# Record count of a projected sequence, one core: broadcast of w over TensorE, last tiles in halves, scans in the tail

## Chip, cores, metric

One core of a Trainium2 chip. The metric is device time in microseconds of one execution, median of several; lower is better. All runs told here were in the fast state. A profile adds a span (first to last instruction), some 1.8 us shorter than the measured time (2.1 us in one kernel, halves_only).

## Reference

```python
def reference(x, w):                      # x: 8 x 2048 x 4096 fp32, w: 4096 x 1 fp32
    proj = (x @ w).squeeze(-1)            # 8 x 2048
    cm = np.maximum.accumulate(proj, axis=1)
    is_record = (proj >= cm).astype(np.float32)
    return np.cumsum(is_record, axis=1).astype(np.float32)
```

x is 268 MB and is read once, each value used once. What follows the projection is a running maximum and a running count over 2048 values in each of 8 sequences.

## The kernel before

x is read in 128 tiles of 128 rows (2.10 MB each) into six buffers. VectorE multiplies each with w, which a broadcast DMA has laid on all 128 partitions, and sums into one column.

```python
w_sb = const.tile([P, D], FP32)
nc.gpsimd.dma_start(out=w_sb, in_=w[:, 0].partition_broadcast(P))   # 2.10 MB
for t in range(T):
    xtile = xpool.tile([P, D], FP32, tag="x")                       # bufs=6
    nc.sync.dma_start(out=xtile, in_=xt[t])
    nc.vector.scalar_tensor_tensor(out=xtile, in0=xtile, scalar=1.0, in1=w_sb,
        op0=ALU.mult, op1=ALU.mult, accum_out=proj_all[:, t : t + 1])
```

Then the tail. proj_all is transposed, so that row t holds the 128 values of tile t. Scans along the rows are made of doubling steps, the carry from row to row goes through a transpose, four more steps in one lane and a transpose back.

```python
projT = copy(transpose(proj_all))
def l1_scan(bufA, bufB, src, op):                 # 7 steps, k = 1, 2, 4 ... 64
    ...
        nc.vector.tensor_tensor(out=nxt[:, PAD:], in0=cur[:, PAD:],
                                in1=cur[:, PAD - k : PAD + P - k], op=op)
def cross_carry(rowval_col, scA, scB, op):
    nc.vector.tensor_copy(out=ZCOL[:, 0:1], in_=rowval_col)
    nc.tensor.transpose(out=p1, in_=ZCOL, identity=ident)
    ...                                           # copy, 4 steps in one lane, copy
    nc.tensor.transpose(out=p2, in_=ZROW, identity=ident)
    return p2[:, 0:1]
cmbuf = l1_scan(MA, MB, projT, ALU.max)
carry_m = cross_carry(last column of cmbuf, ..., ALU.max)
...                                               # compare, 7 steps of add, cross_carry, final add
nc.sync.dma_start(out=out_r, in_=res)
```

## Time and profile before

| quantity | before | from |
|---|---|---|
| time | 659.09 us (4 runs, 658.77 to 659.57); 659.2 to 659.3 beside later runs | timed runs |
| span | 657.2 us | profile |
| first multiply starts | 15.89 us | timeline |
| multiply of the last tile starts | 637.41 us | timeline |
| output DMA issued | 654.63 us | timeline |
| stream rate | 428 GB/s | windows |

The views of this profile are shown and read in the prediction below. In short: DMA sets the pace up to the last tile, VectorE is 88% busy but keeps up, and after the last tile one chain of VectorE and TensorE steps runs with no transfer beside it.

### The profile page before, as it was taken

The page shows a single profiled execution, that of the slowest core. Times are in us where ns is not written, and L with a number is a line of the kernel's source. Part 1 is how long each engine was busy: PE and PEld are TensorE (multiplying, and loading weights), DVE is VectorE, ACT ScalarE, POOL GpSimd, SP SyncE. Part 2 cuts the span into 40 slices and gives each one's busy share as a digit, 9 for nine tenths or more (in the row PEclk, how much of TensorE's full clock was granted, in tenths as well). Part 3 has the DMA queues.
Part 4 walks back from the last instruction along what each step waited for, and adds up shares of the span by engine and source line. Part 5 has one row for each costly group of instructions (what it writes and reads, how often), then busy time and mean ns, then how long its engine had stood idle before and what let it go on. Part 6 is the DMA issues. An engine that isn't in the chain of part 4 may idle for free.

```text
span 657.2 us, 739 instructions
## 1 busy us (share of the span) xinstructions
PE 2.3 (0%) x5; PEld 0.9 (0%) x5; DVE 577.3 (88%) x297; ACT 1.5 (0%) x2; POOL 1.4 (0%) x7
## 2 busy tenths in 40 slices
PE   0000000000000000000000000000000000000001
PEld 0000000000000000000000000000000000000000
DVE  1999898899899899899899899899998899898995
ACT  0000000000000000000000000000000000000000
POOL 0000000000000000000000000000000000000000
DMA  9999999999999999999999999999999999999950
GB/s 366 430 431 428 428 427 427 430 429 430 427 428 427 430 429 429 428 428 428 428 429 428 428 430 429 427 429 430 428 428 429 426 429 430 427 428 429 430 251 4
DMA packets 18725, 270.65 MB, mean 412 GB/s; under 512 B 2080, under 2 KB 2208, under 8 KB 2208
## 3 DMA queue, kind: packets, MB, share of 16 engines
q1 hardware_dynamic: 18576, 268.51, 96.1%
q0 software_dynamic: 144, 2.10, 0.7%
q14 instruction: 5, 0.04, 0.0%
HBM read 270.53 MB, written 0.07 MB: 412 GB/s over the span
## 4 chain that ended last, share of the span: by engine, by line
DMA 82%; DVE 17%; issue 1%; PE 0%; DVEq 0%; ACT 0%; POOLq 0%
DMA xtile<-in_x_dram 79%; DVE xtile L58 16%; DMA w_sb<-in_w_dram 2%; DVE NB L154 0%; DVE MB L103 0%; PE p L116 0%; PE p L135 0%; DVE NA L154 0%; DVE MA L103 0%; DVE SC_S_B L124 0%; DVE SC_M_A L124 0%; DVE SC_M_B L124 0%; DVE SC_S_A L124 0%; PE pt_ps L69 0%; DVE ZROW L133 0%
## 5 line engine op out<-in xcount | busy, mean ns | idle before, releaser
L58 DVE SCALAR_TENSOR_TENSOR xtile<-xtile,w_sb 128x4096 f32<-128x4096 f32 x128 | 566.1, 4425 | 72.2 <-DMA xtile<-in_x_dram 58.8
L58 DVE DVE_READ_ACCUMULATOR xtile<-xtile,w_sb 128x1 f32 x128 | 10.6, 83 | 0.0
L69 PE MATMUL pt_ps<-ident,proj_all 128*128 128x128 f32 x1 | 0.4, 446 | 642.0 <-DVE xtile L58 642.0
L71 ACT COPY projT<-pt_ps 128x128 f32<-128x128 f32 x1 | 0.3, 266 | 640.4 <-PE pt_ps L69 640.4
L103 DVE TENSOR_TENSOR MB<-MA 128x128 f32<-128x128 f32 x4 | 1.2, 292 | 0.1
L154 DVE TENSOR_TENSOR NB<-NA 128x128 f32<-128x128 f32 x4 | 1.2, 292 | 0.1
L71 ACT ACT_TABLE_LOAD x1 | 1.3, 1283 | 0.7 <-PEq L190 0.7
L69 PEld LDWEIGHTS pt_ps<-ident,proj_all 128*128 128x128 f32 x1 | 0.2, 181 | 642.0 <-issue 642.0
L99 DVE COPY MA<-projT 128x128 f32<-128x128 f32 x1 | 0.2, 227 | 0.9 <-ACT projT L71 0.9
L103 DVE TENSOR_TENSOR MA<-MB 128x128 f32<-128x128 f32 x3 | 0.9, 292 | 0.1
L154 DVE TENSOR_TENSOR NA<-NB 128x128 f32<-128x128 f32 x3 | 0.9, 292 | 0.1
L116 PE MATMUL p<-ident,ZCOL 128*128 128x128 f32 x2 | 0.9, 461 | 6.1 <-DVE ZCOL L114 6.1
L142 DVE SCALAR_TENSOR_TENSOR NA<-MB,p,projT 128x128 f32<-128x128 f32 x1 | 0.4, 357 | 0.6 <-PE p L135 0.6
L135 PE MATMUL p<-ident,ZROW 128*128 128x128 f32 x2 | 0.9, 446 | 3.9 <-DVE ZROW L133 3.9
L167 DVE TENSOR_SCALAR res<-NB,p 128x128 f32<-128x128 f32 x1 | 0.3, 292 | 0.6 <-PE p L135 0.6
L79 DVE MEMSET MA<- 128x64 f32 x1 | 0.1, 112 | 0.8 <-PEq L190 0.8
L118 DVE COPY SC_S_A<-p 1x120 f32<-1x120 f32 x1 | 0.3, 270 | 0.6 <-PE p L116 0.6
L118 DVE COPY SC_M_A<-p 1x120 f32<-1x120 f32 x1 | 0.3, 269 | 0.6 <-PE p L116 0.6
L48 POOL DMA_DIRECT2D w_sb<-in_w_dram x1 | 0.7, 660 | 0.8 <-POOLq L190 0.8
L124 DVE TENSOR_TENSOR SC_S_B<-SC_S_A 1x128 f32<-1x128 f32 x2 | 0.6, 280 | 0.1
L124 DVE TENSOR_TENSOR SC_M_B<-SC_M_A 1x128 f32<-1x128 f32 x2 | 0.6, 279 | 0.1
L124 DVE TENSOR_TENSOR SC_M_A<-SC_M_B 1x128 f32<-1x128 f32 x2 | 0.6, 279 | 0.1
(22 smaller groups left out, 4.7 us busy)
## 6 DMA issues: line engine op xcount, KB each, us to landing
xtile<-in_x_dram SPq DMA_DIRECT2D x128, 2048.0 KB, 24.8
w_sb<-in_w_dram POOLq DMA_DIRECT2D x1, 2048.0 KB, 14.6
out_dram<-res SPq DMA_DIRECT2D x1, 64.0 KB, 1.5
```

What stands on the lines that cost most here:

```text
L48: nc.gpsimd.dma_start(out=w_sb, in_=w_flat.partition_broadcast(P))
L58: nc.vector.scalar_tensor_tensor(out=xtile, in0=xtile, scalar=1.0, in1=w_sb, op0=ALU.mult, op1=ALU.mult, accum_out=proj_all[:, t : t + 1],)
L69: nc.tensor.transpose(out=pt_ps, in_=proj_all, identity=ident)
L71: nc.scalar.copy(out=projT, in_=pt_ps)
L103: nc.vector.tensor_tensor(out=nxt[:, PAD:], in0=cur[:, PAD:], in1=cur[:, PAD - k : PAD + P - k], op=op,)
L116: nc.tensor.transpose(out=p1, in_=ZCOL, identity=ident)
L118: nc.vector.tensor_copy(out=scA[:, :, SO + 1 : 2 * SO], in_=rowv[:, :, 0 : SO - 1])
L124: nc.vector.tensor_tensor(out=nxt[:, :, SO:], in0=cur[:, :, SO:], in1=cur[:, :, SO - k : 2 * SO - k], op=op,)
L135: nc.tensor.transpose(out=p2, in_=ZROW, identity=ident)
L142: nc.vector.scalar_tensor_tensor(out=NA[:, PAD:], in0=cmbuf[:, PAD:], scalar=carry_m, in1=projT, op0=ALU.max, op1=ALU.is_le,)
L154: nc.vector.tensor_tensor(out=nxt[:, PAD:], in0=cur[:, PAD:], in1=cur[:, PAD - k : PAD + P - k], op=ALU.add,)
L167: nc.vector.tensor_scalar(out=res, in0=csbuf[:, PAD:], scalar1=carry_s, scalar2=None, op0=ALU.add,)
```

## The change

It aims at both ends of the stream. (1) w is loaded as one row of 16 KB, spread over the partitions by eight fp32 matmuls with a row of ones, and copied to SBUF by ScalarE. (2) The last six tiles are loaded and multiplied in halves, so that less is left to do after the last bytes. (3) The tail uses VectorE's scan instruction, and of the four transposes that carried values from row to row one stays, while two matmuls with one column replace the other three (one of the two with a triangle matrix that sums the row counts). Cut to its core:

```diff
-    nc.gpsimd.dma_start(out=w_sb, in_=w_flat.partition_broadcast(P))
+    nc.scalar.dma_start(out=w_row, in_=w[:, 0][None, :])
+    for j in range(D // MM_N):                     # 8 times 512 columns
+        nc.tensor.matmul(wp, lhsT=ones_row, rhs=w_row[:, j * MM_N : (j + 1) * MM_N], start=True, stop=True)
+        nc.scalar.copy(out=w_sb[:, j * MM_N : (j + 1) * MM_N], in_=wp)
+    LASTT = 6
+    Q = 2
     for t in range(T):
+        if t < T - LASTT: ...                      # whole tile, as before
+        for q in range(Q):
+            cs = slice(q * W, (q + 1) * W)
+            nc.sync.dma_start(out=xtile[:, cs], in_=xt[t][:, cs])
+            nc.vector.scalar_tensor_tensor(out=xtile[:, cs], in0=xtile[:, cs], scalar=1.0,
+                in1=w_sb[:, cs], op0=ALU.mult, op1=ALU.mult,
+                accum_out=parts[:, t - (T - LASTT), q : q + 1])
+    nc.vector.tensor_reduce(out=proj_all[:, T - LASTT :], in_=parts, op=ALU.add, axis=AX.X)
     nc.tensor.transpose(out=pt_ps, in_=proj_all, identity=ident)
-    (copy to SBUF, copy, 7 steps, copy, transpose, copy, 4 steps, copy, transpose)
+    nc.vector.tensor_tensor_scan(out=CM, data0=NEGT, data1=pt_ps, initial=NEG_INF, op0=ALU.max, op1=ALU.max)
+    nc.tensor.transpose(out=p1[0:1, :], in_=CM[:, P - 1 : P], identity=ident)
+    nc.vector.tensor_copy(out=SC[:, :, 1:SO], in_=rowv[:, :, 0 : SO - 1])
+    nc.vector.tensor_tensor_scan(out=ZR, data0=RST..., data1=SC..., initial=NEG_INF, op0=ALU.min, op1=ALU.max)
+    nc.tensor.matmul(p2[:, 0:1], lhsT=ZR, rhs=ones_row[0:1, 0:1], start=True, stop=True)
     (compare)
-    (7 steps, copy, transpose, copy, 4 steps, copy, transpose)
+    nc.vector.tensor_tensor_scan(out=CS, data0=ONES, data1=REC, initial=0.0, op0=ALU.mult, op1=ALU.add)
+    nc.tensor.matmul(p3[:, 0:1], lhsT=Mtri2, rhs=CS[:, P - 1 : P], start=True, stop=True)
     (final add, output)
```

More of the change, by code (lines that the diff above doesn't have):

```diff
@@ L44 @@
     psum = ctx.enter_context(tc.tile_pool(name="psum", bufs=2, space=bass.MemoryType.PSUM))
-    w_sb = const.tile([P, D], FP32)
-    w_flat = w[:, 0]
-    nc.gpsimd.dma_start(out=w_sb, in_=w_flat.partition_broadcast(P))
+    psumw = ctx.enter_context(tc.tile_pool(name="psumw", bufs=4, space=bass.MemoryType.PSUM))
     ident = const.tile([P, P], FP32)
     make_identity(nc, ident)
+    w_row = const.tile([1, D], FP32)
+    nc.scalar.dma_start(out=w_row, in_=w[:, 0][None, :])
+    ones_row = const.tile([1, P], FP32)
@@ new lines @@
+    nc.vector.memset(ones_row, 1.0)
+    w_sb = const.tile([P, D], FP32)
+    MM_N = 512
+    for j in range(D // MM_N):
+        wp = psumw.tile([P, MM_N], FP32, tag="wp")
+        nc.tensor.matmul(
+            wp, lhsT=ones_row, rhs=w_row[:, j * MM_N : (j + 1) * MM_N],
+            start=True, stop=True,
+        )
+        nc.scalar.copy(out=w_sb[:, j * MM_N : (j + 1) * MM_N], in_=wp)
+    Mtri = const.tile([P, B, SO], FP32)
+    nc.gpsimd.memset(Mtri, 1.0)
+    nc.gpsimd.affine_select(
+        out=Mtri, in_=Mtri, compare_op=ALU.is_ge, fill=0.0,
+        base=-1, pattern=[[SO, B], [1, SO]], channel_multiplier=-1,
+    )
@@ L53 @@
+    nc.gpsimd.affine_select(
+        out=Mtri, in_=Mtri, compare_op=ALU.is_ge, fill=0.0,
+        base=0, pattern=[[-SO, B], [0, SO]], channel_multiplier=1,
+    )
+    Mtri2 = Mtri.rearrange("k b j -> k (b j)")
     proj_all = small.tile([P, T], FP32)
+    LASTT = 6
+    Q = 2
+    W = D // Q
+    parts = small.tile([P, LASTT, Q], FP32)
     for t in range(T):
         xtile = xpool.tile([P, D], FP32, tag="x")
-        nc.sync.dma_start(out=xtile, in_=xt[t])
-        nc.vector.scalar_tensor_tensor(
-            out=xtile,
-            in0=xtile,
-            scalar=1.0,
-            in1=w_sb,
-            op0=ALU.mult,
-            op1=ALU.mult,
-            accum_out=proj_all[:, t : t + 1],
-        )
+        if t < T - LASTT:
+            nc.sync.dma_start(out=xtile, in_=xt[t])
+            nc.vector.scalar_tensor_tensor(
+                out=xtile, in0=xtile, scalar=1.0, in1=w_sb,
+                op0=ALU.mult, op1=ALU.mult, accum_out=proj_all[:, t : t + 1],
+            )
+            continue
+        for q in range(Q):
+            cs = slice(q * W, (q + 1) * W)
+            nc.sync.dma_start(out=xtile[:, cs], in_=xt[t][:, cs])
+            nc.vector.scalar_tensor_tensor(
+                out=xtile[:, cs], in0=xtile[:, cs], scalar=1.0, in1=w_sb[:, cs],
+                op0=ALU.mult, op1=ALU.mult,
+                accum_out=parts[:, t - (T - LASTT), q : q + 1],
+            )
@@ L68 @@
+    nc.vector.tensor_reduce(
+        out=proj_all[:, T - LASTT :], in_=parts, op=ALU.add, axis=AX.X,
+    )
     pt_ps = psum.tile([P, P], FP32, tag="tp")
     nc.tensor.transpose(out=pt_ps, in_=proj_all, identity=ident)
-    projT = small.tile([P, P], FP32, tag="projT")
-    nc.scalar.copy(out=projT, in_=pt_ps)
-    PAD = P // 2
-    MA = small.tile([P, PAD + P], FP32, tag="MA")
-    MB = small.tile([P, PAD + P], FP32, tag="MB")
-    NA = small.tile([P, PAD + P], FP32, tag="NA")
-    NB = small.tile([P, PAD + P], FP32, tag="NB")
@@ L79 @@
-    nc.vector.memset(MA[:, :PAD], NEG_INF)
-    nc.vector.memset(MB[:, :PAD], NEG_INF)
-    nc.vector.memset(NA[:, :PAD], 0.0)
-    nc.vector.memset(NB[:, :PAD], 0.0)
-    SC_M_A = small.tile([1, B, 2 * SO], FP32, tag="scma")
-    SC_M_B = small.tile([1, B, 2 * SO], FP32, tag="scmb")
-    SC_S_A = small.tile([1, B, 2 * SO], FP32, tag="scsa")
-    SC_S_B = small.tile([1, B, 2 * SO], FP32, tag="scsb")
-    nc.vector.memset(SC_M_A, NEG_INF)
-    nc.vector.memset(SC_M_B, NEG_INF)
-    nc.vector.memset(SC_S_A, 0.0)
@@ L91 @@
-    nc.vector.memset(SC_S_B, 0.0)
-    ZCOL = const.tile([P, P], FP32)
-    ZROW = const.tile([P, P], FP32)
-    nc.vector.memset(ZCOL, 0.0)
-    nc.vector.memset(ZROW, 0.0)
-    def l1_scan(bufA, bufB, src, op):
-        nc.vector.tensor_copy(out=bufA[:, PAD:], in_=src)
-        cur, nxt = bufA, bufB
-        k = 1
-        while k < P:
-            nc.vector.tensor_tensor(
-                out=nxt[:, PAD:],
-                in0=cur[:, PAD:],
-                in1=cur[:, PAD - k : PAD + P - k],
-                op=op,
-            )
-            cur, nxt = nxt, cur
-            k *= 2
-        return cur
@@ L113, in cross_carry @@
-    def cross_carry(rowval_col, scA, scB, op):
-        nc.vector.tensor_copy(out=ZCOL[:, 0:1], in_=rowval_col)
-        p1 = psum.tile([P, P], FP32, tag="tp")
-        nc.tensor.transpose(out=p1, in_=ZCOL, identity=ident)
-        rowv = p1[0:1, :].rearrange("o (b j) -> o b j", b=B)
-        nc.vector.tensor_copy(
-            out=scA[:, :, SO + 1 : 2 * SO], in_=rowv[:, :, 0 : SO - 1]
-        )
-        cur, nxt = scA, scB
-        k = 1
-        while k < SO:
-            nc.vector.tensor_tensor(
-                out=nxt[:, :, SO:],
-                in0=cur[:, :, SO:],
-                in1=cur[:, :, SO - k : 2 * SO - k],
-                op=op,
-            )
-            cur, nxt = nxt, cur
-            k *= 2
-        zrow_v = ZROW[0:1, :].rearrange("o (b j) -> o b j", b=B)
-        nc.vector.tensor_copy(out=zrow_v, in_=cur[:, :, SO:])
-        p2 = psum.tile([P, P], FP32, tag="tp")
-        nc.tensor.transpose(out=p2, in_=ZROW, identity=ident)
-        return p2[:, 0:1]
@@ L138 @@
-    cmbuf = l1_scan(MA, MB, projT, ALU.max)
-    rowmax = cmbuf[:, PAD + P - 1 : PAD + P]
-    carry_m = cross_carry(rowmax, SC_M_A, SC_M_B, ALU.max)
-    nc.vector.scalar_tensor_tensor(
-        out=NA[:, PAD:],
-        in0=cmbuf[:, PAD:],
-        scalar=carry_m,
-        in1=projT,
-        op0=ALU.max,
-        op1=ALU.is_le,
-    )
-    cur, nxt = NA, NB
-    k = 1
-    while k < P:
-        nc.vector.tensor_tensor(
-            out=nxt[:, PAD:],
-            in0=cur[:, PAD:],
-            in1=cur[:, PAD - k : PAD + P - k],
-            op=ALU.add,
-        )
-        cur, nxt = nxt, cur
-        k *= 2
@@ L162 @@
-    csbuf = cur
-    rowsum = csbuf[:, PAD + P - 1 : PAD + P]
-    carry_s = cross_carry(rowsum, SC_S_A, SC_S_B, ALU.add)
+    NEGT = const.tile([P, P], FP32)
+    ONES = const.tile([P, P], FP32)
+    RST = const.tile([1, B, SO], FP32)
+    SC = const.tile([1, B, SO], FP32)
+    nc.vector.memset(NEGT, NEG_INF)
+    nc.vector.memset(ONES, 1.0)
+    nc.vector.memset(RST, -NEG_INF)
+    nc.vector.memset(RST[:, :, 0:1], NEG_INF)
+    nc.vector.memset(SC, NEG_INF)
+    CM = small.tile([P, P], FP32, tag="CM")
@@ new lines @@
+    REC = small.tile([P, P], FP32, tag="REC")
+    CS = small.tile([P, P], FP32, tag="CS")
+    ZR = small.tile([1, P], FP32, tag="ZR")
+    nc.vector.tensor_tensor_scan(
+        out=CM, data0=NEGT, data1=pt_ps, initial=NEG_INF, op0=ALU.max, op1=ALU.max,
+    )
+    p1 = psum.tile([P, P], FP32, tag="tp")
+    nc.tensor.transpose(out=p1[0:1, :], in_=CM[:, P - 1 : P], identity=ident)
+    rowv = p1[0:1, :].rearrange("o (b j) -> o b j", b=B)
+    nc.vector.tensor_copy(out=SC[:, :, 1:SO], in_=rowv[:, :, 0 : SO - 1])
@@ new lines @@
+    nc.vector.tensor_tensor_scan(
+        out=ZR, data0=RST.rearrange("o b j -> o (b j)"),
+        data1=SC.rearrange("o b j -> o (b j)"),
+        initial=NEG_INF, op0=ALU.min, op1=ALU.max,
+    )
+    p2 = psum.tile([P, P], FP32, tag="tp")
+    nc.tensor.matmul(p2[:, 0:1], lhsT=ZR, rhs=ones_row[0:1, 0:1], start=True, stop=True)
+    nc.vector.scalar_tensor_tensor(
+        out=REC, in0=CM, scalar=p2[:, 0:1], in1=pt_ps, op0=ALU.max, op1=ALU.is_le,
+    )
+    nc.vector.tensor_tensor_scan(
+        out=CS, data0=ONES, data1=REC, initial=0.0, op0=ALU.mult, op1=ALU.add,
+    )
@@ L166 @@
+    p3 = psum.tile([P, P], FP32, tag="tp")
+    nc.tensor.matmul(p3[:, 0:1], lhsT=Mtri2, rhs=CS[:, P - 1 : P], start=True, stop=True)
     res = small.tile([P, P], FP32, tag="res")
     nc.vector.tensor_scalar(
-        out=res,
-        in0=csbuf[:, PAD:],
-        scalar1=carry_s,
-        scalar2=None,
-        op0=ALU.add,
+        out=res, in0=CS, scalar1=p3[:, 0:1], scalar2=None, op0=ALU.add,
     )
```

## The prediction

> **What bounds the kernel now.** I began with the page of the profile: busy shares, the DMA row and the chain that ended last. VectorE is 88% busy and one could take it for the bound, but the chain says otherwise.
>
> ```profile
> PE 2.3 (0%) x5; PEld 0.9 (0%) x5; DVE 577.3 (88%) x297; ACT 1.5 (0%) x2; POOL 1.4 (0%) x7
> ...
> q1 hardware_dynamic: 18576, 268.51, 96.1%
> q0 software_dynamic: 144, 2.10, 0.7%
> q14 instruction: 5, 0.04, 0.0%
> ...
> DMA 82%; DVE 17%; issue 1%; PE 0%; DVEq 0%; ACT 0%; POOLq 0%
> ...
> L58 DVE SCALAR_TENSOR_TENSOR xtile<-xtile,w_sb 128x4096 f32<-128x4096 f32 x128 | 566.1, 4425 | 72.2 <-DMA xtile<-in_x_dram 58.8
> ```
>
> The reader is to see that the chain is 82% DMA; that x and the broadcast w (q0, 2.10 MB, as large as one x tile) share the same 16 engines; and that the 128 multiplies wait 58.8 us for x. A multiply takes 4.43 us, but in the timeline they start every 4.90 us: 2.097 MB in 4.898 us is 428 GB/s, the stream's rate. So VectorE has 0.47 us to spare in each tile and the stream sets the pace. The windows view gives three regimes (its last two columns are DMA share and GB/s):
>
> ```profile
> 0.00:10.00 10.00, 0.00 (x0) 0.00 (x0) 1.69 (x10) 1.28 (x1) 1.38 (x7) 1.00 0.83 319
> 10.00:20.00 10.00, 0.00 (x0) 0.00 (x0) 4.11 (x1) 0.00 (x0) 0.00 (x0) 1.00 1.02 437
> ...
> 30.00:630.00 600.00, 0.00 (x0) 0.00 (x0) 542.06 (x245) 0.00 (x0) 0.00 (x0) 1.00 1.01 428
> 630.00:640.00 10.00, 0.00 (x0) 0.00 (x0) 9.12 (x5) 0.00 (x0) 0.00 (x0) 1.00 0.41 174
> 640.00:657.00 17.00, 2.26 (x5) 0.91 (x5) 10.32 (x33) 0.27 (x1) 0.00 (x0) 1.00 0.01 4
> ```
>
> From about 1.7 to 634 us the engines are full; after that the kernel is a serial tail without DMA. The timeline shows both ends of VectorE's work: the first multiply held until w has landed, and the tail after the last tile.
>
> ```profile
> 15.89 4.43 DVE L58 SCALAR_TENSOR_TENSOR xtile<-xtile,w_sb 128x4096 f32<-128x4096 f32 x1 [13.36 <-DMA w_sb<-in_w_dram]
> ...
> 637.41 4.43 DVE L58 SCALAR_TENSOR_TENSOR xtile<-xtile,w_sb 128x4096 f32<-128x4096 f32 x1 [0.41 <-DMA xtile<-in_x_dram]
> 641.76 0.08 DVE L58 DVE_READ_ACCUMULATOR xtile<-xtile,w_sb 128x1 f32 x1
> 641.96 0.18 PEld L69 LDWEIGHTS pt_ps<-ident,proj_all 128*128 128x128 f32 x1 [641.96 <-issue]
> 641.99 0.45 PE L69 MATMUL pt_ps<-ident,proj_all 128*128 128x128 f32 x1 [641.99 <-DVE xtile L58]
> 642.47 0.27 ACT L71 COPY projT<-pt_ps 128x128 f32<-128x128 f32 x1 [640.44 <-PE pt_ps L69]
> ...
> 654.31 0.29 DVE L167 TENSOR_SCALAR res<-NB,p 128x128 f32<-128x128 f32 x1 [0.63 <-PE p L135]
> 654.63 0.35 SPq L175 DMA_DIRECT2D out_dram<-res  x1
> ```
>
> So the time is: stream until the last tile lands (637.3), 4.5 us for its multiply, 12.8 us from there (641.84) to the issue of the output (654.63), 2.6 us to the end of the span (657.2), and 1.9 us between span and measured time (659.09). The chance to gain lies at those places; what happens while the stream runs counts only if it stops the stream.
>
> [...]while w was in flight (1.2 to 15.9 us) the total was no higher than later (437 against 428 GB/s), so w's 2.10 MB was taken from x.[...]
>
> **The change, part by part.**
>
> *The broadcast of w.* Removed: 2.10 MB[...], which is exactly one tile period, 4.90 us. Added: 16 KB on the ScalarE queue, under 0.1 us of stream. All x tiles should land 4.9 us earlier. **-4.9 us**, on the path, if the stream never runs dry. Would it? Six tiles are issued at once; the stream begins at about 1.7 us, so with 0.7 us of ramp it lasts until 1.7 + 0.7 + 6 x 4.9 = 31.8. The seventh tile is issued when the first multiply ends, and needs about 0.9 us from issue to first bytes (0.75 to 1.65 at the start). So the first multiply must start before about 31.8 - 0.9 - 4.5 = 26 us. When is the new w ready? The row lands at, say, 4 to 8 us (it has to take turns with x). Then eight fp32 matmuls of 512 columns[...]. ScalarE copies beside them, one of some 0.6 us left over at the end. Ready at 12 to 23 us: maybe later than the 15.9 of now, and still in time. VectorE then starts with a backlog, works it off at 4.90 - 4.35 = 0.55 us a tile (back to back they start 4.35 us apart) and is abreast after some twenty tiles. So a later first multiply costs nothing.
>
> *The last six tiles in halves.* A half's multiply takes [...]2.29 us, two of them 4.4 us back to back, still under 4.90. Only the last half is on the path: from landing to accumulator 2.3 us in place of 4.43, **-2.1 us**. Its price: rows of 8 KB and six more completions, for which I put +0.1 us, and one small reduction, which I count in the tail.
>
> *The tail.* Steps of the chain before were taken from the timeline: DVE end to DVE start across a TensorE transpose 0.63 us, gap between two VectorE operations 0.03. New chain from the last accumulator: reduction of 12 values a lane 0.20; transpose 0.62; scan straight from PSUM 0.46; transpose of the last column 0.62; copy of 120 values 0.30 (it was 0.27); scan over 128 in one lane 0.46; matmul with one column 0.6 (not measured here[...]); compare 0.41 (it was 0.36[...]); scan 0.45; matmul with one column 0.6; final add 0.32. Sum 5.04 us against 12.79 now. **-7.75 us**. What goes is 7 + 7 steps of 0.33 and 4 + 4 steps of 0.31, two copies through ScalarE and VectorE, and the four copies that fill and empty the padded rows; what comes are three scans. The memsets of constants ran in the first 3 us before and I expect them there again; if they stay behind the loop they hide behind the first transpose.
>
> Sum: 659.09 - 4.9 - 2.1 + 0.1 - 7.75 = 644.4 us, 2.2% less. The limit of 2% is near 646.
>
> **Rivals.** (A) *The row of w comes late*: it waits behind the x tiles queued first, or the matmuls are slower than I think, the first multiply starts after 26 us and the stream runs dry. For it: SP has issued some megabytes of x by then. Against it: in the kernel before, w on another queue got about half of the bandwidth beside the same six x tiles (2.10 MB within 14.6 us). Each us beyond 26 costs one; if the row had to wait for all six tiles (some 32 us, w ready at 45) the time would be 664, slower than now.
> (B) *The w saving is hidden*: the last landing is set by something other than bytes. For it: of the 16 engines the mean is done at 634, but the last tile lands at 637.3, so one or two engines end about 3 us behind. I looked at the spacing of the multiplies: it is 4.90 throughout, except longer steps near 112, 195, 313 to 318 and 525 us, and the instruction queue's five packets fall in just those windows. These hiccups add up to 2.3 us. [...]I take them as unchanged, with 1 us either way. [...]If only half came off: 646.9.
> (C) *Scans and small matmuls dearer*: if a scan went at 4 cycles a value (0.7 us) and an fp32 matmul hop took 0.9 us, the tail would be 6.5 us: 645.9, right at the limit.
> (D) *Halves disturb the stream*: 8 KB pieces with gaps in memory. If the last six tiles lost 5% of the rate: +1.5 us, 645.9.
> (E) *Better*: the lag of the slowest engine comes partly from the software queue of w, and the ramp (319 GB/s in the first 10 us) is smoother without it: up to 2 us less, 642.4.
>
> **Range and chances.** The tail I know within 1 us, the stream within 1.5. Predicted 644.4; eight times in ten between 642.4 and 647.2, more room above, since A, B, C and D all point up. Faster by over 2% needs less than about 646: 0.75. Within 2%: 0.22. Slower by over 2% needs rival A in full: 0.03.
>
> **What will show it.** Right: in the DMA part no software queue, 268.6 MB in all; the last x landing at about 632.5; the last multiply 2.29 us; from last accumulator to the output's issue about 5.0 us; scans of about 424 ns; a first multiply between 12 and 23 us, then back to back for twenty tiles without an effect on the end. Wrong: DMA share under 0.9 around 32 us (A); a last landing above 634.5 (B, D); scans above 600 ns or TensorE hops above 0.9 us (C); a last landing below 631.5 (E).

## The result, and the profile after

644.63 us (median of 8 runs, 644.27 to 644.82) against 659.18 (13 runs) beside it: 14.55 us or 2.2% less. The ratio is 0.978, 95% interval 0.977 to 0.979. A ratio here is one of fast runs over fast runs, with the 95% interval of the record.

The page of the kernel after, the lines that answer to those shown of before:

```profile
PE 15.9 (2%) x22; PEld 6.4 (1%) x22; DVE 569.4 (89%) x281; ACT 6.0 (1%) x9; POOL 1.5 (0%) x9
...
q1 hardware_dynamic: 19440, 268.51, 98.3%
q14 instruction: 6, 0.04, 0.0%
q10 hardware_dynamic: 2, 0.02, 0.0%
...
L94 DVE SCALAR_TENSOR_TENSOR xtile<-xtile,w_sb 128x2048 f32<-128x2048 f32 x12 | 26.9, 2287 | 0.7 <-DMA xtile<-in_x_dram 0.5
```

The software queue with its 2.10 MB is gone; in its place q10 carries 0.02 MB in two packets. A half's multiply takes 2287 ns, as expected (2.29 us; the straight line through 292 ns for 128 elements and 4425 ns for 4096, both measured in the kernel before, gives 2292 for 2048). Next the windows of the kernel after (the last two columns are again DMA share and GB/s):

```profile
10.00:20.00 10.00, 8.07 (x10) 2.66 (x8) 1.27 (x1) 3.10 (x6) 0.00 (x0) 1.00 1.01 431
...
30.00:600.00 570.00, 0.00 (x0) 0.00 (x0) 520.61 (x237) 0.00 (x0) 0.00 (x0) 1.00 1.01 428
600.00:630.00 30.00, 0.00 (x0) 0.00 (x0) 29.18 (x23) 0.00 (x0) 0.00 (x0) 1.00 1.00 417
630.00:640.00 10.00, 1.68 (x6) 1.10 (x6) 7.29 (x12) 0.00 (x0) 0.00 (x0) 1.00 0.03 11
```

The stream goes at 428 GB/s as before; in the stretch of the halves it is a little slower. (That window also holds the end of the stream; from 600 to 625 us, in steps of 5 us, it reads 419 to 423.) The timeline of the kernel after, both ends:

```profile
4.08 13.99 PE L58 MATMUL wp<-w_row,ones_row 1*128 1x512 f32 x16 [4.08 <-DMA w_row<-in_w_dram]
...
18.73 4.42 DVE L86 SCALAR_TENSOR_TENSOR xtile<-xtile,w_sb 128x4096 f32<-128x4096 f32 x1 [17.09 <-ACT w_sb L62]
...
625.93 2.29 DVE L94 SCALAR_TENSOR_TENSOR xtile<-xtile,w_sb 128x2048 f32<-128x2048 f32 x1 [0.23 <-DMA xtile<-in_x_dram]
...
633.26 2.29 DVE L94 SCALAR_TENSOR_TENSOR xtile<-xtile,w_sb 128x2048 f32<-128x2048 f32 x1
635.48 0.08 DVE L94 DVE_READ_ACCUMULATOR xtile<-xtile,w_sb 128x1 f32 x1
635.60 0.17 DVE L99 TENSOR_REDUCE proj_all<-parts 128x6 f32<-128x12 f32 x1
...
636.39 0.42 DVE L120 TENSOR_TENSOR_SCAN CM<-NEGT,pt_ps 128x128 f32<-128x128 f32 x1 [0.63 <-PE pt_ps L104]
...
637.58 0.41 DVE L127 TENSOR_TENSOR_SCAN ZR<-RST,SC 1x128 f32<-1x128 f32 x1
...
638.73 0.35 DVE L134 SCALAR_TENSOR_TENSOR REC<-CM,p,pt_ps 128x128 f32<-128x128 f32 x1 [0.74 <-PE p L133]
639.12 0.42 DVE L137 TENSOR_TENSOR_SCAN CS<-ONES,REC 128x128 f32<-128x128 f32 x1
...
640.29 0.29 DVE L144 TENSOR_SCALAR res<-CS,p 128x128 f32<-128x128 f32 x1 [0.74 <-PE p L141]
640.61 0.35 SPq L148 DMA_DIRECT2D out_dram<-res  x1
```

The reader is to see three things. The first multiply starts later than before (18.73 against 15.89 us), since w comes through the matmuls, and yet the last multiply starts 4.15 us earlier (633.26 against 637.41). That multiply is 2.14 us shorter. From its accumulator (635.56) to the issue of the output it is 5.05 us, where it was 12.79.

### The profile page after: what moved, and what is told of

Its sections match the earlier page's. It is cut to its first block, busy times and chain, and to the rows that moved or that the text cites. A ratio compares the mean times of both kernels' runs of the same rounds, so it can differ in the third digit from the quotient of the medians.

```text
span 643.0 us, 774 instructions
## 1 busy us (share of the span) xinstructions
PE 15.9 (2%) x22; PEld 6.4 (1%) x22; DVE 569.4 (89%) x281; ACT 6.0 (1%) x9; POOL 1.5 (0%) x9
## 4 chain that ended last, share of the span: by engine, by line
DMA 73%; DVE 20%; issue 4%; PE 2%; ACT 0%; DVEq 0%; SPq 0%
DMA xtile<-in_x_dram 73%; DVE xtile L86 19%; PE wp L58 2%; DMA w_row<-in_w_dram 0%; DVE xtile L94 0%; ACT w_sb L62 0%; PE p L141 0%; PE p L133 0%; PE pt_ps L104 0%; DVE CS L137 0%; DVE CM L120 0%; DVE ZR L127 0%; PE p L124 0%; DVE REC L134 0%; DVEq L86 0%
## 5 line engine op out<-in xcount | busy, mean ns | idle before, releaser
L86 DVE SCALAR_TENSOR_TENSOR xtile<-xtile,w_sb 128x4096 f32<-128x4096 f32 x122 | 538.6, 4425 | 66.9 <-DMA xtile<-in_x_dram 49.9
L94 DVE SCALAR_TENSOR_TENSOR xtile<-xtile,w_sb 128x2048 f32<-128x2048 f32 x12 | 26.9, 2287 | 0.7 <-DMA xtile<-in_x_dram 0.5
L58 PE MATMUL wp<-w_row,ones_row 1*128 1x512 f32 x16 | 14.0, 1064 | 4.1 <-DMA w_row<-in_w_dram 4.1
L58 PEld LDWEIGHTS wp<-w_row,ones_row 1*128 1x128 f32 x16 | 5.1, 329 | 11.4 <-issue 9.3
L62 ACT COPY w_sb<-wp 128x512 f32<-128x512 f32 x8 | 4.7, 587 | 11.4 <-PE wp L58 11.4
```

Source lines behind the costliest of these rows:

```text
L58: nc.tensor.matmul(wp, lhsT=ones_row, rhs=w_row[:, j * MM_N : (j + 1) * MM_N], start=True, stop=True,)
L62: nc.scalar.copy(out=w_sb[:, j * MM_N : (j + 1) * MM_N], in_=wp)
L94: nc.vector.scalar_tensor_tensor(out=xtile[:, cs], in0=xtile[:, cs], scalar=1.0, in1=w_sb[:, cs], op0=ALU.mult, op1=ALU.mult, accum_out=pa ...
```

## The experiments

The theory is the sum of the prediction: three savings that don't touch each other (bytes of the stream, the last piece of work, the chain of the tail), and a first multiply that is free as long as the queue of x doesn't run dry. Its rivals: the saving of w comes from giving up the software queue and not from the bytes; the late first multiply costs part of it; the halves do something other than shorten the last multiply. Twelve runs were made; the time beside each is of the kernel before in the same call.

**One part alone, three kernels.** Each is the kernel before with one of the three parts.

```diff
 tail_only:    old broadcast, old loop, the new tail
 w_only:       new broadcast, old loop, old tail
 halves_only:  old broadcast, loop with LASTT = 6 halves and the reduction, old tail
```

> The kernel before with the new tail alone (scans, small matmuls), old broadcast of w and whole tiles. Theory (the three savings are separate and add up): the last x still lands at 637.3 us of the span, from the last accumulator to the output's issue 4.85 us (5.04 without the reduction of the halves, which this kernel does not need), so 659.2 - 7.95 = 651.2 us. Rival (the tail gains only together with the halves, or the scans disturb the stream): last landing later than 638, time above 653.

> The kernel before with the new broadcast of w alone. Theory (w's bytes cost the stream one tile period, less 0.4 us that the traces of before and after show lost at the head): 659.2 - 4.5 = 654.7 us, the first multiply at about 18.7 us and the later start without effect on the end. Rival (VectorE's later start costs part of it): 656 or more. Rival (the saving of w is hidden): 659.

> The kernel before with the last six tiles in halves alone. Theory: last multiply 2.29 instead of 4.43 (-2.14), a reduction on the path (+0.2), the last six tiles streaming 0.4 us slower: 659.2 - 1.55 = 657.65 us. Rival (halves cost the stream nothing, the 0.4 us lost between the 122nd tile and the end came from the new w): 657.25.

Measured beside 659.24 us: tail_only 651.23 us (ratio 0.988), w_only 654.18 us (0.992), halves_only 657.91 us (0.998). That is 8.01, 5.06 and 1.33 us, in sum 14.40, against 14.55 for all three together. The parts add up to well within the 95% intervals (about 0.16% of the time, or 1 us, to each side for the first two); no rival here holds. The last multiply of w_only:

```profile
632.73 4.42 DVE L69 SCALAR_TENSOR_TENSOR xtile<-xtile,w_sb 128x4096 f32<-128x4096 f32 x1 [0.42 <-DMA xtile<-in_x_dram]
```

In the traces the last multiply starts at 637.72 us in tail_only and at 632.73 in w_only, so the scans don't move the stream, and the first multiply at 17.86 us in w_only cost nothing. One number of the trace is blurred: up to the last whole tile before the halves (the 122nd multiply), single profiles of kernels with the old broadcast differ by 0.3 us (608.08, 608.38 and 608.41), so the saving by w, 4.5 us between the first two traces, is 4.8 us between the mean of these three and that of six traces with the new one (603.5).

The cost of the halves is sharp, though. From the 122nd multiply to the last it is 29.33 to 29.34 us in four kernels with whole tiles, and 29.70 to 29.73 in the five kernels with six tiles in halves (six traces): 0.38 us for six split tiles, 0.06 us each. So the halves won 2.14 - 0.38 - 0.2 (the reduction) = 1.56 us by the trace, and 1.33 were timed. The record shows where the difference is: the spans of halves_only's 13 runs are 1.68 us shorter than those of the kernel before beside them (655.79 against 657.48 on average), but its time exceeds its span by 2.1 us, where the other kernels have 1.7 to 1.8. So 0.34 us of the gain were lost outside the span in this kernel alone; why, no run shows.

**The queue or the bytes.**

```diff
-    nc.gpsimd.dma_start(out=w_sb, in_=w_flat.partition_broadcast(P))
+    nc.scalar.dma_start(out=w_sb, in_=w_flat.partition_broadcast(P))
```

> The kernel before, its 2.10 MB broadcast of w issued on ScalarE's hardware queue in place of GpSimd's software queue; nothing else. Theory (the bytes cost the time, not the queue): 659.2 within 0.5 us. Rival (the software queue slows engines or the ramp): down to 655 to 657.

Measured: 658.57 us against 659.24 (0.999, interval 0.9981 to 0.9998). The same bytes over the hardware queue gain 0.67 us by the medians (0.1 to 1.25 by the interval), just past the half microsecond that the theory allowed; the other 4.4 of the 5.06 us of w_only come only when the bytes go. The bytes are the main cause; the software queue has a small share. The 4.4 us are half a microsecond short of the tile period of 4.90. By the windows w_hw_queue moved 14.08 MB in its first 35 us and w_only 13.94, which is worth 0.3 us of the stream; the rest is open.

**How late may the first multiply be?**

```diff
-        nc.tensor.matmul(wp, ...)
+        for _ in range(2 if j < 3 else 1):      # w_late_5; w_late_14: range(2) for every j
+            nc.tensor.matmul(wp, ...)
```

> The changed kernel with the first three of the eight broadcast matmuls done twice, so that w is ready 5.1 us later and the first multiply starts at 23.9 us. Theory (a late first multiply is free until about 26 us, when six queued tiles run out): 644.6 us, unchanged. Rival (the start of VectorE's work counts): 649.7 us or some part of the 5 us.

> The changed kernel with all eight broadcast matmuls done twice; the first multiply starts at 32.4 us. Theory: the stream runs dry at about 31.8 us and starts again about 0.9 us after the first multiply ends (36.8), so it loses 6 us: 650.6 us, with a stretch of near-zero DMA share from 32 to 37 us. Rival (the delay counts in full): 658.3. Rival (free as well): 644.6.

Measured beside 659.34: w_late_5 644.58 us, with its first multiply at 23.00; w_late_14 650.86 us, with its first multiply at 31.65. Both as the theory had them, and the rivals (5 and 14 us, or nothing) are out. The windows of w_late_14 show the queue running dry (DMA share and GB/s at the end of a line):

```profile
31.00:32.00 1.00, 0.00 (x0) 0.00 (x0) 0.35 (x1) 0.58 (x1) 0.00 (x0) 1.00 0.74 311
32.00:33.00 1.00, 0.00 (x0) 0.00 (x0) 1.00 (x1) 0.00 (x0) 0.00 (x0) 1.00 0.01 0
...
36.00:37.00 1.00, 0.00 (x0) 0.00 (x0) 1.00 (x3) 0.00 (x0) 0.00 (x0) 1.00 0.00 0
37.00:38.00 1.00, 0.00 (x0) 0.00 (x0) 1.00 (x1) 0.00 (x0) 0.00 (x0) 1.00 1.37 279
```

All six tiles are in by 32 us, none can be asked for until the first multiply frees its buffer at 36, and the stream stands for five microseconds; the last multiply of this kernel starts 6.2 us later than that of the kernel after. 13.6 us of extra TensorE work cost 6.2 us, and in w_late_5 another 5.1 us cost nothing. The slack is what the prediction worked out from six buffers; the number of buffers itself was not varied.

**How many tiles in halves?**

```diff
-    LASTT = 6
+    LASTT = 1        # halves_last;  2: halves_2;  T (all 128): halves_all
```

> The changed kernel with only the last tile in halves in place of the last six. Theory (each split tile costs the stream 0.06 us, 0.37 over six): 644.3 us. Rival (the 0.37 us is one step at the change to halves, or chance): 644.6.

> The changed kernel with all 128 tiles in halves, to make that cost large. Theory (0.06 us for each split tile): 122 more of them, +7.5 us, 652.1 us, the stream at 421 instead of 428 GB/s throughout. VectorE needs 4.43 us for two halves, still less than the 4.96 us of a tile. Rival (one step): 644.6.

Measured beside 659.34: halves_last 646.16 us, halves_all 655.82 us. Both expectations missed, and the first was wrong in sign: 644.3 was expected, and one split tile is 1.5 us slower than six. The timeline of halves_last says why:

```profile
628.15 4.43 DVE L86 SCALAR_TENSOR_TENSOR xtile<-xtile,w_sb 128x4096 f32<-128x4096 f32 x1 [0.47 <-DMA xtile<-in_x_dram]
632.50 0.08 DVE L86 DVE_READ_ACCUMULATOR xtile<-xtile,w_sb 128x1 f32 x1
632.50 2.29 DVE L94 SCALAR_TENSOR_TENSOR xtile<-xtile,w_sb 128x2048 f32<-128x2048 f32 x1
...
634.72 2.29 DVE L94 SCALAR_TENSOR_TENSOR xtile<-xtile,w_sb 128x2048 f32<-128x2048 f32 x1
```

The last whole tile lands just before 628.15 and holds VectorE until 632.50. Both halves follow at once: the first starts together with the accumulator read of the whole tile (632.50), the second 2.22 us later, and neither shows a wait in brackets. So VectorE, not the stream, is the bound at the end. An estimate from these rows and from the price of a split tile: halves land every 2.48 us (4.90 + 0.06 a tile), VectorE takes 4.35 for the whole tile and then 2.21 for each half. The first half could start 2.48 after the whole tile and starts 4.35 after it; each further half makes up 2.48 - 2.21 = 0.27. VectorE is abreast (it waits for x again) after eight halves, four tiles. In the kernel after, with six, the first halves run back to back in the same way and the waits for x come back with the ninth half, at 625.93, as shown above. This new theory was put to a test of its own:

> The changed kernel with the last two tiles in halves in place of six. Theory (the last whole tile puts VectorE behind: it takes 4.35 us from its landing while halves land every 2.48; each half works off 0.27 us, so four halves leave it 4.35 + 3 x 2.21 - 4 x 2.48 = 1.06 us late at the last one, against 1.60 us with one split tile; four fewer split tiles give the stream back 4 x 0.06): 644.6 + 1.06 - 0.25 = 645.4 us, all four halves back to back. Rival (the loss with one split tile has to do with the last tile alone, so two are enough): 644.35.

Measured: 645.82 us beside 644.65 us for the kernel after in the same call (after_again, told below). All four halves ran back to back, from 627.40 to 634.03 at 2.21 us, and the last one started 0.74 us later than in the kernel after (633.29), where 0.8 was worked out. The rival (644.35) is out. The time differs by 1.17 us, where 0.8 was expected (645.4 us). Up to the output's issue the difference stays 0.74 us; the rest of 0.4 us arises after it, about 0.25 of it between the output's issue and the end of the span, and its cause stays open.

halves_all was to enlarge the stream's price of 0.06 us a tile. The stream ran at 422 GB/s throughout instead of 428, from the windows of halves_all:

```profile
300.00:400.00 100.00, 0.00 (x0) 0.00 (x0) 91.65 (x81) 0.00 (x0) 0.00 (x0) 1.00 1.01 422
```

Between late steps two halves take 4.97 us where a tile took 4.90 (4.971 and 4.896 on average), 0.075 us for each of 122 more tiles, or 9.2 us where 7.5 were expected; so it is a lasting price and not one step. Of the other 2 us, 0.25 are a longer reduction (0.42 us in place of 0.17), and 1.6 lie in a few single late steps of the multiplies, which in sum delay by 3.9 us in this kernel, by 2.1 in the kernel before and by 2.3 in the kernel after. There are eight packets of the instruction queue in this kernel, which has 122 more loads and multiplies than the kernel after, and five and six in those two; in the kernel before the five packets fall in the same windows as the late steps (near 112, 195, 313 to 318 and 525 us). That is a coincidence in time, seen in the traces and tested by no run. The price of the halves itself, whether it belongs to the 8 KB rows or to the completions, was not taken apart.

**The row of w in pieces, and a try at a better version.** The row of 16 KB, if it runs on one DMA engine, occupies it for 0.6 us (an estimate: the 128 rows of a tile pass in 4.90 us over the 16 engines that the page counts, so one row in 4.90 / 8 if they are spread evenly). Its queue shows two packets, which fits that; no view shows the engines singly. w_spread loads it as 16 pieces of 1 KB. quarters takes that and changes the ends: four tiles in halves and the last three in quarters. after_again is the kernel after, for the same chip and rounds.

```diff
-    w_row = const.tile([1, D], FP32)
-    nc.scalar.dma_start(out=w_row, in_=w[:, 0][None, :])
+    w_row = const.tile([1, 16, 264], FP32)       # padded rows: the pieces can't be merged
+    nc.scalar.dma_start(out=w_row[:, :, 0:256], in_=w[:, 0][None, :].rearrange("o (a f) -> o a f", a=16))
 quarters, besides:
-    LASTT = 6
+    NH, NQ = 4, 3                                # 4 tiles in halves, then 3 in quarters
```

> The changed kernel once more, unaltered, as the reference for the other three of this call: 644.6 us within 0.3.

> The changed kernel with the 16 KB row of w loaded as 16 pieces of 1 KB[...]. Theory (the one packet holds up one engine by 0.6 us, but that need not be the engine that ends last): 644.2 us, between 644.0 and 644.6, with 32 packets on that queue. Rival (it matters fully): 644.0. Rival (the pieces slow every engine): 645.

> A try at a version that beats both: spread row of w, then four tiles in halves (enough to let VectorE catch up) and the last three in quarters. Theory: the last multiply falls from 2.29 to 1.22 us (-1.07); the stream pays 4 x 0.06 + 3 x 0.2 in place of 0.38 (+0.46); VectorE takes 4 x 1.15 = 4.6 us for four quarters, just under a tile period, so it is abreast at the end or nearly: 643.9 us. Rival (VectorE does not get abreast, or quarters of 4 KB rows slow the stream more): 644.6 or more.

Measured: after_again 644.65 us (644.47 to 644.74), w_spread 644.99 (644.70 to 645.08), quarters 644.30 (644.18 to 644.36). The pieces were not merged, 32 packets on that queue, but they made it no faster, by the medians rather 0.3 us slower, with ranges that just overlap. That is the number of the second rival, and 0.24 us of it are there by the 121st multiply (598.90 against 598.66; the other kernels with whole tiles up to there and the new w have 598.50 to 598.77); whether every engine was slowed, as that rival has it, no run shows. And the row came later. The first matmul of w_spread:

```profile
7.63 1.19 PE L61 MATMUL wp<-w_row,ones_row 1*128 1x512 f32 x1 [7.63 <-DMA w_row<-in_w_dram]
```

It starts at 7.63 us, and in quarters at 7.51, where the row in one piece allowed 3.02 to 4.25 in eight traces (4.08 in the kernel after). Why the pieces came later, no run shows. Since w is not urgent (a first multiply at 23.00 us cost nothing in w_late_5), the later start is harmless, and the theory's gain of up to 0.6 us didn't come. What holds back the last bytes (a DMA share of 0.18, 0.06 and 0.04 from 630 to 633 us in the kernel after) was not shown.

In quarters the last multiply is 1.22 us and starts at 633.92, 0.63 later than the last half of after_again: 1.07 won, 0.63 given back to a slower stream (410 GB/s between 620 and 628 us) and to w_spread's 0.3. The expected 643.9 us were missed by 0.4. By the medians it is the fastest kernel of the study, 0.35 us ahead of the kernel after in the same call, or 0.05%; the runs of the two in that call don't overlap (the first eight runs of the kernel after, 644.27 to 644.82, do overlap with it), and the gain is too small to matter. Quarters without the spread row were not run.

## Why the prediction was right

- **The bound.** DMA up to the last tile, then a chain. Confirmed: each part moved the piece of the timeline it was said to move, and the parts add up (14.40 against 14.55 us).
- **w, -4.9.** Timed 5.06 alone. The mechanism was in the main the bytes, as said, but they were worth 4.4 us on the same queue, not 4.9; the queue's 0.7, the small true part of rival E, made up for it, and that is luck. The reading that w's bytes came out of those of x holds: from 10 to 20 us the rate is 437 GB/s with w beside x (in flight up to 15.9) and 436 in w_only without it. One reading under rival A is off: w's 2.10 MB were not half of what moved while w was in flight but about 36% (5.8 MB up to 15.9 us, by the windows); nothing hung on it, since the new row was there at 4.08 us.
- **A late first multiply is free up to about 26 us.** Right: 23.0 is free, 31.65 costs 6.2; a cost of 1 us for each us beyond it would put the limit at 25.4, and no run lies between. VectorE was abreast after 18 tiles, where some twenty were said. The range given for it, 12 to 23 us, was the author's estimate, since no trace before the change shows such matmuls; 18.73 lay in it. The eight fp32 matmuls took 1.71 us each, 14.0 in all, and ScalarE's copies 587 ns each. Rival A's mechanism is real, as w_late_14 shows; its threshold was not reached.
- **Halves, -2.1 + 0.1.** The gain was right (2.14). The price was too low: 0.38 us, not 0.1, because it was put down without a source. The working was also incomplete: "Only the last half is on the path" holds only since enough tiles are split for VectorE to catch up; the prediction did not work out that six are enough, so this came right by luck. With one or two it fails, as halves_last and halves_2 show. The prediction checked that two halves fit into a tile period and did not ask what the whole tile before them leaves behind.
- **The tail, 5.04 us.** Measured 5.05, but with misses that cancel: the transpose of one column took 0.47 us from VectorE to VectorE instead of 0.62, the two matmuls with one column 0.74 each instead of 0.6 (the trace shows each as two instructions), and the other steps were together 0.1 shorter; the scans, 420, 411 and 425 ns, came out at the author's estimate (424), for which no trace before the change showed a scan.
- **The last landing.** Expected near 632.5, and the last multiply started at 633.26: 0.3 of it is the halves' price, 0.4 what the head of this trace shows less than 4.9. The time came out at 644.63 for 644.4 all the same because the end after the output's issue was 0.2 us shorter (2.4 for 2.6) and the difference between span and median time 0.26 us smaller (1.63 for 1.89), of which 0.17 is only where the two profiled runs lay beside their medians. Neither was foreseen; that is luck too. So a total that is right within 0.3 us does not mean terms that are right within 0.3.

## What to carry to other kernels

In a stream that DMA bounds, look at what comes before the first byte, what bytes go along that need not, and what runs after the last byte; work inside the stream was free here up to the slack that the buffers hold (a first multiply at 23.00 us cost nothing, one at 31.65 us cost 6.2 us), and in this case that slack came out of queue depth and tile period. Splitting the last transfer to shorten what follows worked in full here only when the consuming engine was abreast of the stream at that point (644.63 us with six tiles split, 645.82 with two, 646.16 with one): count how many split pieces it takes to make up for the last whole one. A serial chain of small steps is worth its count: replacing 22 steps of 0.31 to 0.33 us by three of 0.42 was the largest part of this gain (the whole new tail alone: 8.01 us).

## What the traces measured of the hardware

- One row of 16 KB on ScalarE's queue went as 2 packets, and beside the stream of x it was usable at 3.0 to 4.3 us; loaded as 16 pieces it was usable at 7.5 to 7.6 us.
- VectorE's scalar-tensor-tensor on two fp32 operands in SBUF, with the accumulator, took 4425 ns for 4096 elements and 2287 ns for 2048. The plain fp32 tensor-tensor step of 128 elements took 292 ns, and the scan of 128 elements 411 to 425 ns.
- The fp32 matmuls of one row by 512 columns came as pairs of instructions 0.853 us apart, 1.71 us a matmul, from the first to the last, and in w_late_14 over 27.6 us without any speed-up. The profile gives the granted clock as 1.00 all the while; what sets the 1.71 us, no run shows.
- Rows of 8 KB in place of 16 KB, with twice as many loads, cost the saturated stream 0.06 to 0.08 us per 2.10 MB tile (422 against 428 GB/s).
- Late steps of 0.1 to 1.0 us coincide with the packets of the instruction queue, in sum 2.1 us in the kernel before. No run tested whether the packets cause them.
